# The start of the wide matmuls' operands: 96 bytes past a multiple of 128, or on one

## The chip, the cores and the metric

The kernel runs on one core of a Trainium2 chip. A core has a matrix engine (TensorE, in the profile PE, with its weight loads as PEld), VectorE (DVE), ScalarE (ACT), GpSimd (POOL) and SyncE (SP), which issues nearly all transfers. The metric is the device time of one execution in microseconds.

## What is computed

One layer of a decoder trunk over 2048 tokens of width 1024, in float32. An input projection feeds two groups of token mixers (four heads of a gated delta rule, four of HGRN2, each with 128 x 128 states); an output projection, a squared-ReLU MLP of width 4096 and a gated per-layer embedding follow, with RMS norms between:

```python
hn = rms_norm(h, pre_mix_norm[i])
proj = jnp.einsum('btd,dc->btc', hn, w_in[i])
...
o_a = gated_delta_rule_chunked(q_a, k_a, v_a, g_dec, beta)
o_b = hgrn2_chunked(jax.nn.silu(q_hg), k_b, i_hg, log_f)
...
h = h + rms_norm(jnp.einsum('btc,cd->btd', mix, w_out[i]), post_mix_norm[i])
u = jnp.einsum('btd,df->btf', rms_norm(h, pre_mlp_norm[i]), w_mlp_up[i])
y = jnp.einsum('btf,fd->btd', jnp.square(jax.nn.relu(u)), w_mlp_down[i])
h = h + rms_norm(y, post_mlp_norm[i])
e = rms_norm(jnp.einsum('bte,ed->btd', p[i], w_ple_proj[i]), ple_norm[i])
gate = jax.nn.sigmoid(jnp.einsum('btd,de->bte', h, w_ple_gate[i]))
h = h + e * gate
```

## The kernel before

Everything is held transposed, with features in the 128 partitions and tokens along a partition, 512 tokens at a time. Each large product is made from matmuls of a 128 x 128 stationary operand with a moving operand of 128 partitions by 512 columns. Both are float32r tiles that hold a number in two parts, the rounded value and the rest; three matmuls (high by high, high by low, low by high) stand for one float32 product:

```python
terms += [(w[:, 0, k, :], xk[:, 0, :]), (w[:, 0, k, :], xk[:, 1, :]), (w[:, 1, k, :], xk[:, 0, :])]
```

There are 10,344 such wide matmuls in the program, and 48 more with 256 columns in the last output tile. The rest are narrow ones in plain float32, most of them with 128 columns or fewer, in the mixers.

The stages follow one another in time. First come the embedding projection (tiles `mme`) and the norms of the first tokens. Then, up to about 1012 us, the input projection (`mm`, line 1176) runs with the mixers' narrow matmuls put in between: each of 132 projections has 24 wide matmuls in three steps of eight, and after each step a table of offsets says which part of which mixer is issued. Then the output projection (`mmo`), the MLP's up product (`u`) and down product (`d`), both in seven products instead of eight with sums on VectorE, and the gate (`mmg`), all through line 1210. TensorE's order is the order of the code; in the MLP SyncE's is too. VectorE and ScalarE prepare the split operands and take the results out of the accumulators.

Where an operand starts is decided by the pools. A pool is a stretch of each partition; pools are laid one behind another from the left, or, with `side="right"`, from the other end. Tiles are rounded up to 32 bytes, so an address is the sum of what was allocated ahead. Four pools hold the operands of wide matmuls. `ra` is a ring of ten moving tiles of 4096 bytes, behind the small constants of `cp`. `wp` holds stationary tiles at the right end while the mixers run, and `bp` takes its place in the MLP. `rb` is a second ring of 18 moving tiles, opened after the mixers where their tiles were, and the tiles of the pool `b2` (the same use as `bp`) lie behind it. A pool `pad` with one tile that nothing uses stands ahead of `rb`:

```python
cp = ctx.enter_context(tc.tile_pool(name="cp", bufs=1))                                    # 102
ra = ctx.enter_context(tc.tile_pool(name="ra", bufs=10))                                   # 103
wp = wctx.enter_context(tc.tile_pool(name="wp", bufs=3, side="right"))                     # 105
...
ctx.enter_context(tc.tile_pool(name="pad", bufs=1)).tile([P, 48], F32, name="pad")         # 1194
second.append(ctx.enter_context(tc.tile_pool(name="rb", bufs=18, reuse_waits="tile")))     # 1195
```

In the built program the first tile of `ra` starts at byte 18144 of its partition, the first of `rb` at 81888, and the stationary tiles at 204768 and the like: each is 96 bytes past a multiple of 128. The parts inside a tile start a multiple of 512 bytes further on, so all operands of the wide matmuls, stationary and moving, have that remainder.

Of the kernel before, what the change touches and what calls it, by code (L numbers as in the profile page):

```python
# [10 lines left out]
F32 = mybir.dt.float32  # L11
# [9 lines left out]
P = 128  # L21
# [75 lines left out]
def trunk(ctx, tc, x, xT, pT, vecs, w_in, w_ab, gdn_a_log, gdn_dt_bias, w_out, w_up, w_down,  # L97
# [2 lines left out]
    V, S, G, PE = nc.vector, nc.scalar, nc.gpsimd, nc.tensor  # L100

    cp = ctx.enter_context(tc.tile_pool(name="cp", bufs=1))
    ra = ctx.enter_context(tc.tile_pool(name="ra", bufs=10))
    wctx = ctx.enter_context(ExitStack())
    wp = wctx.enter_context(tc.tile_pool(name="wp", bufs=3, side="right"))
    st = ctx.enter_context(tc.tile_pool(name="st", bufs=2))
# [1084 lines left out]

    pp = ctx.enter_context(tc.tile_pool(name="pq", bufs=4, space=PSUM))
    po = ctx.enter_context(tc.tile_pool(name="pr", bufs=2, space=PSUM))
    ctx.enter_context(tc.tile_pool(name="pad", bufs=1)).tile([P, 48], F32, name="pad")
    second.append(ctx.enter_context(tc.tile_pool(name="rb", bufs=18, reuse_waits="tile")))
    f2 = ctx.enter_context(tc.tile_pool(name="f2", bufs=1, reuse_waits="tile"))
    octx = ctx.enter_context(ExitStack())
# [791 lines left out]
```

## Time and profile before

| | |
|---|---|
| median of 3 runs | 2643.54 us (2637.11 to 2644.09) |
| span of the profiled execution | 2639.5 us, 4.0 us under that median |
| TensorE busy | 2602.8 us, 15593 matmul records |
| VectorE, ScalarE, GpSimd busy | 1965.0, 1463.3, 137.0 us |
| moved by DMA | 573.87 MB, 217 GB/s on the mean |

The span goes from the first to the last instruction of the profiled execution. The profile gives no time of that execution beside it; the timed runs stand in the first row. Busy time of TensorE counts from each matmul's start to a modelled end, and neighbouring matmuls overlap, so the time that one costs is read from the distance between starts. A plain float32 matmul appears as two records, a float32r one as one.

### The profile page before, as it was taken

What the parts mean: (1) busy time and instruction counts of PE and PEld (TensorE: products, weight loads), DVE (VectorE), ACT (ScalarE), POOL (GpSimd) and SP (SyncE); (2) the same over time, 40 slices, a digit from 0 to 9 for tenths busy, and PEclk for the clock granted to TensorE, in tenths of its full rate; (3) what the DMA queues carried; (4) which work ended last, traced back from release to release, by engine and by line L of the source; (5) the groups of instructions that cost most, each with busy time, mean ns of one, the idle gap of its engine ahead of it and who ended that gap; (6) DMA issues with size and microseconds to landing.
All of it is one profiled execution on the core that took longest, in us unless ns stands there. A gap on an engine that the chain in (4) does not pass through costs nothing.

```text
span 2639.5 us, 43913 instructions
## 1 busy us (share of the span) xinstructions
PE 2602.8 (99%) x15593; PEld 2146.0 (81%) x15593; DVE 1965.0 (74%) x4032; ACT 1463.3 (55%) x2991; POOL 137.0 (5%) x147
## 2 busy tenths in 40 slices
PE   8999999999999999999999999999999999999999
PEld 6778788878878888787888888888888888888887
DVE  7778777776777777579988768767877765477775
ACT  7766655465555555566666465555454465565431
POOL 0000000000000000110000000001000001101000
PEclk9999999999999999999999999999999999999999
DMA  8877777767767675764675576665644375677663
GB/s 277 282 258 265 263 256 245 238 222 251 241 213 240 222 237 162 232 203 141 214 236 182 179 233 223 214 211 186 220 150 168 140 245 187 202 252 251 207 223 126
DMA packets 267788, 573.87 MB, mean 217 GB/s; under 512 B 55578, under 2 KB 60152, under 8 KB 250416
## 3 DMA queue, kind: packets, MB, share of 16 engines
q1 hardware_dynamic: 265264, 566.86, 64.5%
q0 software_dynamic: 2304, 4.20, 0.9%
q8 instruction: 123, 2.02, 0.3%
q14 instruction: 97, 0.79, 0.1%
HBM read 410.57 MB, written 160.37 MB: 216 GB/s over the span
## 4 chain that ended last, share of the span: by engine, by line
PE 61%; DMA 2%; issue 2%; DVE 2%; ACT 0%; POOL 0%; SPq 0%; DVEq 0%; POOLq 0%; ACTq 0%
PE d L1210 23%; PE u L1210 23%; PE mmg L1210 7%; PE mm L1176 4%; PE mmo L1059 1%; PE mme L203 1%; DMA yod<-yo 1%; DMA mixT<-mixd 0%; DMA rsb_g<-rd_g 0%; DMA yo<-in_xT_dram 0%; DVE t L177 0%; DMA rd_g<-m_g 0%; DVE acc_o L246 0%; POOL yo L1296 0%; DMA raw_out<-in_w_out_dram 0%
## 5 line engine op out<-in xcount | busy, mean ns | idle before, releaser
L1176 PE MATMUL mm<-xt,w 128*128 128x512 f32 x3072 | 785.5, 401 | 1.6 <-DVE acc_vg L571 0.7
L1176 PEld LDWEIGHTS mm<-xt,w 128*128 128x128 f32 x3072 | 552.8, 188 | 108.3 <-issue 2.1
L1210 PE MATMUL d<-db,da 128*128 128x512 f32 x2688 | 612.8, 389 | 0.0
L1210 PE MATMUL u<-t,wu 128*128 128x512 f32 x2604 | 591.2, 389 | 0.0
L1210 PEld LDWEIGHTS d<-db,da 128*128 128x128 f32 x2688 | 504.5, 188 | 104.8
L1210 PEld LDWEIGHTS u<-t,wu 128*128 128x128 f32 x2604 | 488.7, 188 | 101.5
L230 DVE TENSOR_TENSOR db<-db 128x512 fp32r<-128x512 f32 x224 | 159.5, 712 | 60.0 <-ACT db L229 59.0
L1612 DVE TENSOR_TENSOR u<-u,u 128x512 f32<-128x512 f32 x224 | 150.2, 681 | 52.0 <-PE u L1210 50.4
L229 ACT ACTIVATE db<-db 128x512 fp32r<-128x512 f32 x224 | 140.9, 629 | 67.4 <-DMA db<-hid 63.6
L1210 PE MATMUL mmg<-h2T,wg 128*128 128x512 f32 (+1 forms) x792 | 174.7, 383 | 0.0
L1210 PEld LDWEIGHTS mmg<-h2T,wg 128*128 128x128 f32 x792 | 145.5, 188 | 29.1
L1655 ACT ACTIVATE u<-u 128x512 f32<-128x512 f32 x128 | 80.7, 631 | 152.8 <-DVE u L1612 152.1
L177 DVE TENSOR_TENSOR da<-da 128x512 fp32r<-128x512 f32 x128 | 95.2, 743 | 91.3 <-ACT da L176 89.5
L176 ACT ACTIVATE da<-da 128x512 fp32r<-128x512 f32 x128 | 80.6, 630 | 127.8 <-DMA da<-sumd 100.9
L1210 PE MATMUL mmo<-mixT,w_out 128*128 128x512 f32 x600 | 140.0, 393 | 3.3 <-ACT w_out L176 2.0
L1210 PEld LDWEIGHTS mmo<-mixT,w_out 128*128 128x128 f32 x600 | 113.4, 190 | 28.8 <-DVE w_out L177 2.6
L176 ACT ACTIVATE wu<-a 128x512 fp32r<-128x512 f32 x124 | 75.0, 623 | 55.8 <-DMA a<-in_w_up_dram 52.9
L177 DVE TENSOR_TENSOR wu<-a,wu 128x512 fp32r<-128x512 f32 x124 | 85.9, 694 | 8.3 <-ACT wu L176 8.2
L177 DVE TENSOR_TENSOR da<-dr,da 128x512 fp32r<-128x512 f32 x96 | 68.2, 711 | 23.7 <-ACT da L176 22.2
L1656 ACT ACTIVATE u<-u 128x512 f32<-128x512 f32 x128 | 80.4, 628 | 3.0
L176 ACT ACTIVATE da<-dr 128x512 fp32r<-128x512 f32 x96 | 60.5, 630 | 31.9 <-DMA dr<-in_w_down_dram 21.7
L246 POOL TENSOR_TENSOR acc_y<-acc_y,sq_y 128x512 f32<-128x512 f32 x28 | 37.8, 1351 | 759.5 <-ACT sq_y L245 759.5
(401 smaller groups left out, 3675.4 us busy)
## 6 DMA issues: line engine op xcount, KB each, us to landing
w<-cache_in SPq DMA_DIRECT2D x96, 1024.0 KB
db<-hid SPq DMA_DIRECT2D x224, 256.0 KB
cache_in<-w SPq DMA_DIRECT2D x32, 1024.0 KB
hid<-u SPq DMA_DIRECT2D x128, 256.0 KB
da<-sumd SPq DMA_DIRECT2D x128, 256.0 KB
a<-in_w_up_dram SPq DMA_DIRECT2D x124, 256.0 KB
hid<-ht SPq DMA_DIRECT2D x96, 256.0 KB
dr<-in_w_down_dram SPq DMA_DIRECT2D x96, 256.0 KB
```

The lines of the kernel that those rows point to most:

```text
L176: S.activation(t[:, 0], raw, AF.Copy)
L177: eng.tensor_tensor(t[:, 1], raw, t[:, 0], ALU.subtract)
L203: PE.matmul(ps, a, b, start=i == 0, stop=i == n - 1)
L229: S.activation(t[:, 0], plain(t), AF.Copy)
L230: V.tensor_tensor(t[:, 1], plain(t), t[:, 0], ALU.subtract)
L246: eng.tensor_tensor(acc, acc, sq, ALU.add)
L1059: PE.matmul(ps, w[:, term // 2, k, :], xin[q][k][:, term % 2, :], start=i == 0, stop=i == 3 * KD - 1)
L1176: PE.matmul(ps, *terms[i], start=i == 0, stop=i == nt - 1)
L1210: PE.matmul(ps, a, b, start=start, stop=stop)
L1612: V.tensor_tensor(c[new], c[old], ps, ALU.add)
L1655: S.activation(c[k], c[k], AF.Relu)
L1656: S.activation(c[k], c[k], AF.Square)
```

## The change

A tile of 32 bytes is added to `cp`, ahead of `ra`; a tile of 96 bytes is put at the right end, ahead of `wp`; and the tile of `pad` shrinks from 192 to 64 bytes. Nothing reads or writes these tiles. Every other allocation keeps its size and order.

```diff
     cp = ctx.enter_context(tc.tile_pool(name="cp", bufs=1))
+    cp.tile([P, 8], F32, name="even")
     ra = ctx.enter_context(tc.tile_pool(name="ra", bufs=10))
+    ctx.enter_context(tc.tile_pool(name="edge", bufs=1, side="right")).tile([P, 24], F32, name="edge")
     wctx = ctx.enter_context(ExitStack())
...
-    ctx.enter_context(tc.tile_pool(name="pad", bufs=1)).tile([P, 48], F32, name="pad")
+    ctx.enter_context(tc.tile_pool(name="pad", bufs=1)).tile([P, 16], F32, name="pad")
```

In the built program `ra` now starts at byte 18176, `rb` at 81792, and the stationary tiles named above at 204672, all multiples of 128. What lies between `ra` and `rb` (the tiles of the mixers, the norms and the staging) moves up by 32 bytes with `ra`. The instructions, their order on each engine and the semaphores that they wait for are the same.

## The prediction

> **What bounds the kernel now.** I read the page's head and busy shares first, then the list of what TensorE waits for, then the groups of its instructions, and then its instructions in order of time, to get the distance from one matmul to the next. The page says that TensorE is the bound nearly everywhere, at a granted clock of nine tenths or more in every slice:
>
> ```profile
> span 2639.5 us, 43913 instructions
> PE 2602.8 (99%) x15593; PEld 2146.0 (81%) x15593; DVE 1965.0 (74%) x4032; ACT 1463.3 (55%) x2991; POOL 137.0 (5%) x147
> PEclk9999999999999999999999999999999999999999
> ```
>
> The span leaves 36.7 us in which TensorE ran nothing. The list of its waits opens with one at the very start (pT), and falls to a few microseconds at once; the last column is the longest single wait:
>
> ```profile
> PE mme L203 <- ACT pT L176: 9.4, 2, 7.1
> PE of_g L633 <- ACT y_qg L580: 2.5, 3, 1.0
> PE mmo L1210 <- ACT w_out L176: 2.0, 1, 2.0
> PE psa_g L820 <- DVE S_g L832: 1.9, 4, 0.6
> ```
>
> So a change in the time per matmul reaches the end of the kernel, and a change elsewhere doesn't. Nearly all of that work is one shape, 128 rows by 512 columns. The groups by shape (count, busy us, mean ns, idle before):
>
> ```profile
> L1176 PE MATMUL mm<-xt,w 128*128 128x512 f32 x3072 | 785.5, 401 | 1.6 <-DVE acc_vg L571 0.7 <-DVE w L177 0.5 <-DVE acc_kg L571 0.4
> L1210 PE MATMUL d<-db,da 128*128 128x512 f32 x2688 | 612.8, 389 | 0.0
> L1210 PE MATMUL u<-t,wu 128*128 128x512 f32 x2604 | 591.2, 389 | 0.0
> L1210 PE MATMUL mmg<-h2T,wg 128*128 128x512 f32 x744 | 169.0, 389 | 0.0
> L1210 PE MATMUL mmo<-mixT,w_out 128*128 128x512 f32 x600 | 140.0, 393 | 3.3 <-ACT w_out L176 2.0 <-DVE w_out L177 1.3
> L633 PE MATMUL of_g<-y_kg 128*32 128x96 f32 x64 | 7.3, 248 | 0.0
> L952 PE MATMUL pss_h<-v_h,hk_h 128*128 128x128 f32 x128 | 16.9, 275 | 0.0
> L1210 PE MATMUL mmg<-h2T,wg 128*128 128x256 f32 x48 | 5.9, 283 | 0.0
> ```
>
> The mean of 389 ns is the time from a matmul's start to its modelled end; neighbours overlap, so it isn't the price. The price is the distance between starts. Three merged rows of the instructions in order of time give it (start us, us from first start to last end, count at the end):
>
> ```profile
> 1661.80 38.47 PE L1210 MATMUL d<-db,da 128*128 128x512 f32 x169
> 2629.21 5.91 PE L1210 MATMUL mmg<-h2T,wg 128*128 128x256 f32 x48
> 140.19 1.06 PE L952 MATMUL pss_h<-v_h,hk_h 128*128 128x128 f32 x8
> ```
>
> Take off the last one's own duration and divide by the number of steps: 512 columns (38.47 - 0.389) / 168 = 226.7 ns; 256 columns (5.91 - 0.283) / 47 = 119.7 ns; 128 columns of plain float32 (1.06 - 0.275) / 7 = 112.1 ns.
>
> **The change, part by part.** It adds or removes no instruction and no wait; it moves tiles by 32 bytes up (everything allocated from the left before the second ring), by 96 bytes down (the second ring and what follows it, and everything allocated from the right). In the built programs all 10,344 matmuls of 512 columns (9,708 in the five groups above, 636 in smaller ones), and the 48 of 256, start at 96 past a multiple of 128 bytes before and at a multiple after, with both of their operands. The two new tiles are never written or read, and cost nothing: no engine and no DMA touches them.
>
> *The wide matmul.* From 256 to 512 columns the distance grows by 107.0 ns, so a column costs 0.418 ns. 512 columns would then take 214.0 ns and 256 columns 107.0 ns: both widths show the same 12.7 ns on top. What could those be? A run of 2048 bytes that starts 96 bytes past a multiple of 128 touches 17 pieces of 128 bytes, a run of 1024 bytes touches 9; from a multiple of 128 they touch 16 and 8. One piece is 32 columns, 32 x 0.418 = 13.4 ns. If a matmul that takes one column per step can't hide the piece that it reads too much, both widths pay about 13 ns, which is what they show; pieces of 64 bytes would make 33 instead of 32, or 6.7 ns, and that isn't what stands there. The third row agrees: plain float32 takes 275 - 248 = 27 ns for 32 columns, 0.84 ns each, half the pace; at that pace five pieces for four (67 ns) hide under 107 ns of columns, and only 112.1 - 107.0 = 5.1 ns remain, less than half of the 12.7. So I take the extra piece for real. What the trace can't show is what is left when it is gone. Bounds: nothing left (saving 12.7 ns, the whole remainder), or the 5.1 ns of the narrow matmul, the nearest row of a matmul that isn't held by its reads (saving 7.6 ns). Neither row is nearer; I take the middle, some 2.5 ns left, a saving of 10.2 ns.
>
> [...]
>
> Sum: 10,344 x 10.2 ns = 105.5 us, and 48 x 10.2 ns = 0.5 us, together 106 us; at the ends 10,392 x 12.7 = 132 us and 10,392 x 7.6 = 79 us. The weight loads (81% busy, beside the matmuls) get the same shift; they are hidden, 188 ns inside 226.7, and stay inside 216:
>
> ```profile
> L1210 PEld LDWEIGHTS d<-db,da 128*128 128x128 f32 x2688 | 504.5, 188 | 104.8
> ```
>
> I count nothing for them, and nothing for the narrow matmuls. If that cover went, the excess of a load over a matmul would come on top, and there is none as long as the distance stays above 188 ns.
>
> *What is given back.* With TensorE faster, what was just in time is late. Two stages decide:
>
> ```profile
> 88.00:1020.00 932.00, 919.69 (x7977) 759.63 (x7975) 711.22 (x2051) 539.61 (x1422) 53.12 (x61) 1.00 0.73 243
> 1188.00:1452.00 264.00, 262.68 (x1157) 216.56 (x1156) 236.13 (x382) 161.76 (x273) 0.00 (x0) 1.00 0.58 193
> 1254.00:1320.00 66.00, 66.00 (x293) 54.63 (x292) 61.51 (x102) 40.06 (x67) 0.00 (x0) 1.00 0.65 215
> 2000.00:2270.00 270.00, 270.00 (x1193) 1.00 0.56 188
> ```
>
> (Columns: stretch, its us, then busy us and count of PE, PEld, DVE, ACT and POOL, the clock, the share of the DMA engines, GB/s; the last row is of PE alone.) The first is the mixers. There 396 steps of 8 wide matmuls stand between the narrow ones, which wait for VectorE and ScalarE in a chain. Each step gets 8 x 10.2 = 82 ns shorter. TensorE is idle 932 - 919.7 = 12.3 us there, in short waits like those listed above, so few steps wait today, but some do. If in one step of four the result comes after the shortened step, 99 x 82 ns = 8 us are given back. The bounds are 0 and the whole 32 us of these steps. The second is the start of the MLP: VectorE is busy 236.1 of 264 us there, 27.9 us over for 382 instructions, 73 ns each. In its fullest part, 1254 to 1320 us, 61.5 of 66 us are busy and 4.5 us lie between 102 instructions, 44 ns each; I take that as what it needs. TensorE would want this part in 66 - 293 x 0.0102 = 63.0 us, VectorE can't do it under 66.0, so 3 us are given back; over the whole stretch TensorE wants 252.2 us and VectorE 236.1 + 382 x 0.044 = 252.9, about even. Bounds 0 and all 12 us. After 1452 us VectorE has room (the last row's stretch: TensorE without a gap, and 10.2 ns of 226.7 is 4.5%). The transfers:
>
> ```profile
> GB/s 277 282 258 265 263 256 245 238 222 251 241 213 240 222 237 162 232 203 141 214 236 182 179 233 223 214 211 186 220 150 168 140 245 187 202 252 251 207 223 126
> DMA packets 267788, 573.87 MB, mean 217 GB/s; under 512 B 55578, under 2 KB 60152, under 8 KB 250416
> ```
>
> In a span 4% shorter 217 GB/s become 226, and the first slices already hold 277 to 282; I count nothing for them.
>
> 106 - 11 = 95 us. On the profile's span: 2639.5 - 95 = 2544.5 us; the median of the runs, 2643.54, is 4.0 us above that span, and I keep the 4.0: **2548.5 us**, 3.6% less.
>
> **The rivals.** *More is given back.* If the mixers keep their pace (32 us lost) and the stage from 1188 to 1452 too (12 us), 62 us remain: 2581.5 us; with the small end of the saving, 79 - 44 = 35 us: 2608. For it speaks that the mixers' narrow matmuls stand in a chain through three engines, one after another; against it, that VectorE is busy only 711 of 932 us there (76%), and that the waits listed come to few microseconds.
>
> *No change.* The 12.7 ns belong to every wide matmul, whatever its address: the change of the weights, say, costs a fixed time. For it: it is the same at both widths, and all wide matmuls before have one alignment, so that the trace has no other to compare. Against it: a fixed price per instruction should show on the narrow ones, which load weights for each matmul as well, and those show 5.1 ns. It gives 2643.5 us, within 0.3%. [...]
>
> *Slower.* The same shift moves the operands of VectorE and ScalarE. If an address class that is good for TensorE is bad for VectorE, its instructions get longer, and the place where that decides is the stretch from 1188 to 1452 us: it has 73 ns for each of 382 instructions there. Above that VectorE is the bound: at 100 ns more each, 382 x 0.027 = 10 us there and, with no gain on TensorE, 2654 us. Against it: it would take 15% of an instruction of 681 ns, the commonest one there, and TensorE without a gain:
>
> ```profile
> L1612 DVE TENSOR_TENSOR u<-u,u 128x512 f32<-128x512 f32 x224 | 150.2, 681 | 52.0 <-PE u L1210 50.4
> ```
>
> That the change doesn't do what it says is excluded by the addresses of the built programs, named above.
>
> **How the numbers follow.** The forecast (the piece is saved, little given back) 0.67; more given back 0.13; no change 0.14; slower 0.06. Runs of this kernel lie between 2637.1 and 2644.1 us, so 0.3% is about what can be told from no change. The first two are faster: 0.80; same 0.14; slower 0.06. The range goes from the whole 132 us with nothing given back, 2511, a little under it for the rounding of the rows, to the far end of the second case, 2608: 2508 to 2608 us. That leaves out the last two cases, 2 in 10.
>
> **What would show it.** In the profile after, the run of d-matmuls should show 214 to 219 ns from start to start instead of 226.7, the 256-column ones 107 to 112 instead of 119.7, and the plain float32 ones no change within 2 ns. The stretch from 2000 to 2270 us should hold some 1250 matmuls instead of 1193. The mean of VectorE's and ScalarE's instructions should stay, their shares rise by 3 to 4%. TensorE's idle time should grow from 36.7 us to some 48, in the mixers above all. I am wrong on the cause if the distance stays at 226.7 ns, wrong on the size if it comes out under 214 or above 219, and wrong on what is given back if the sum of TensorE's waits grows by more than 20 us or not at all.

## The result, and the profile after

The changed kernel takes 2657.26 us (median of 4 runs, 2655.01 to 2659.55), the kernel before 2643.82 (4 runs, 2637.11 to 2644.60): 1.0058 times as long, with an interval of 1.0041 to 1.0074. It is slower by about 0.6%; forecast was a gain of 3.6%. The head of the page after shows where it went, in the same lines as before:

```profile
span 2655.9 us, 43913 instructions
PE 2622.1 (99%) x15593; PEld 2145.2 (81%) x15593; DVE 1963.3 (74%) x4032; ACT 1465.0 (55%) x2991; POOL 137.4 (5%) x147
PEclk9999999999999999999999999999999999999999
```

The span grew by 16.4 us, TensorE's busy time by 19.3 us, at the same granted clock (0.999 and 1.000 on the mean) and with the same instructions; VectorE and ScalarE stayed within 2 us. So TensorE is still the bound, and its own work got longer. The groups by shape tell which part (count, busy us, mean ns, idle before; lines lie 2 further down than before):

```profile
L1178 PE MATMUL mm<-xt,w 128*128 128x512 f32 x3072 | 795.6, 404 | 1.2 <-DVE acc_vg L573 0.9 <-DVE acc_qg L573 0.2
L1212 PE MATMUL d<-db,da 128*128 128x512 f32 x2688 | 613.1, 389 | 0.0
L1212 PE MATMUL u<-t,wu 128*128 128x512 f32 x2604 | 599.3, 392 | 0.0
L1212 PE MATMUL mmg<-h2T,wg 128*128 128x512 f32 x744 | 170.6, 391 | 0.0
```

`mm` went from 785.5 to 795.6 us and `u` from 591.2 to 599.3, while `d`, with nearly as many matmuls of the same shape, stayed (612.8 to 613.1). The change put all operands on multiples of 128 bytes, so alignment alone can't divide `u` from `d`. Distances from start to start, as in the prediction (runs of `u` before, then of `d` and `u` after, in order of time):

```profile
1840.41 38.92 PE L1210 MATMUL u<-t,wu 128*128 128x512 f32 x171
```
```profile
1666.66 43.68 PE L1212 MATMUL d<-db,da 128*128 128x512 f32 x192
1850.51 38.79 PE L1212 MATMUL u<-t,wu 128*128 128x512 f32 x168
```

`u` before: (38.92 - 0.389) / 170 = 226.7 ns. After: `d` (43.68 - 0.389) / 191 = 226.7 ns, `u` (38.79 - 0.392) / 167 = 229.9 ns. No run of wide matmuls fell below 226.7 ns, and some became slower.

What divides them are the pools, seen modulo 256 instead of 128. Before, every wide operand starts 224 bytes past a multiple of 256. After, the first ring `ra` (18176) starts on a multiple of 256, and the stationary tiles (204672) and the second ring `rb` (81792) 128 past one. The moving operand lies in `ra` for all matmuls of `mm` and for a part of `mmo`, `u`, `mmg` and `mme` (960 of the 2688 of `u`); but for 48 of `mme`, whose weights lie in `ra` too, their two operands are now 128 bytes apart, modulo 256. The operands of `d`, and those of the matmuls fed from `rb`, still have equal starts. The experiments test whether this distance is the cause.

### The profile page after: what moved, and what is told of

Same layout as the page of the kernel before. It is cut to its first block, busy times and chain, and to the rows that moved or that the text cites. A ratio compares the mean times of both kernels' runs of the same rounds, so it can differ in the third digit from the quotient of the medians.

```text
span 2655.9 us, 43913 instructions
## 1 busy us (share of the span) xinstructions
PE 2622.1 (99%) x15593; PEld 2145.2 (81%) x15593; DVE 1963.3 (74%) x4032; ACT 1465.0 (55%) x2991; POOL 137.4 (5%) x147
## 4 chain that ended last, share of the span: by engine, by line
PE 68%; DVE 3%; DMA 3%; issue 2%; ACT 1%; SPq 0%; POOL 0%; DVEq 0%; ACTq 0%; POOLq 0%
PE u L1212 23%; PE d L1212 23%; PE mm L1178 9%; PE mmg L1212 7%; PE mmo L1061 1%; PE mme L205 1%; DMA yod<-yo 1%; DMA mixT<-mixd 0%; DMA sys_g<-ud_g 0%; DVE t L179 0%; DVE acc_o L248 0%; PE psb_g L827 0%; PE psa_g L822 0%; DMA yo<-in_xT_dram 0%; PE of_g L836 0%
## 5 line engine op out<-in xcount | busy, mean ns | idle before, releaser
L1178 PE MATMUL mm<-xt,w 128*128 128x512 f32 x3072 | 795.6, 404 | 1.2 <-DVE acc_vg L573 0.9
L1212 PE MATMUL d<-db,da 128*128 128x512 f32 x2688 | 613.1, 389 | 0.0
L1212 PE MATMUL u<-t,wu 128*128 128x512 f32 x2604 | 599.3, 392 | 0.0
L1614 DVE TENSOR_TENSOR u<-u,u 128x512 f32<-128x512 f32 x224 | 150.2, 681 | 60.6 <-PE u L1212 59.6
```

The costliest lines, as they stand in the source:

```text
L1178: PE.matmul(ps, *terms[i], start=i == 0, stop=i == nt - 1)
L1212: PE.matmul(ps, a, b, start=start, stop=stop)
L1614: V.tensor_tensor(c[new], c[old], ps, ALU.add)
```

## Experiments

The theories: *piece*, the prediction's (only each start's place within 128 bytes counts, and the kernel lost its gain elsewhere); *place* (a start has a good or bad place modulo 256 by itself); *pair* (the distance between the starts of the moving and the stationary operand counts, modulo 256). Below, "distance" is the start of the stationary operand minus that of the moving one, modulo 256.

**The price by start, by itself.** A kernel that only multiplies: 64 groups of 25 float32r matmuls of 512 columns, the moving operand starting at m x 32 bytes, the stationary one at s x 32 bytes, m and s from 0 to 7 (letters a to h in the names).

```diff
+    PE.matmul(ps, sta[:, 8 * s : 8 * s + P], mov[:, 8 * m : 8 * m + QT], start=i == 0, stop=i == n - 1)
```

> Leaves the whole computation out: 64 groups of 25 wide float32r matmuls, the moving operand starting 0, 32, ... 224 bytes past a multiple of 256 (letter a to h after m) and the stationary one likewise (letter after s), nothing beside them. Pair theory (the distance between the two starts modulo 256 sets the price): 226.7 ns from start to start in the 8 groups where both letters are equal, some 233 ns where they are four letters (128 bytes) apart, whatever the first letter; others unknown, between 214 and 240. Place theory (a moving operand that begins on a multiple of 256 is slow): the groups of ma are slow (233 ns) with every stationary start, those of mh at 226.7 with every one. Piece theory of the prediction (an extra 128-byte piece): ma and me at 214 to 219, all others 226.7.

Its instructions in order of time (start us, us, name with m and s, count):

```profile
21.29 5.84 PE L36 MATMUL masa<-mov,sta 128*128 128x512 f32 x25
26.96 5.99 PE L36 MATMUL masb<-mov,sta 128*128 128x512 f32 x25
...
44.47 5.97 PE L36 MATMUL mase<-mov,sta 128*128 128x512 f32 x25
50.28 6.00 PE L36 MATMUL masf<-mov,sta 128*128 128x512 f32 x25
...
206.86 6.00 PE L36 MATMUL mesa<-mov,sta 128*128 128x512 f32 x25
212.69 6.00 PE L36 MATMUL mesb<-mov,sta 128*128 128x512 f32 x25
...
230.10 5.84 PE L36 MATMUL mese<-mov,sta 128*128 128x512 f32 x25
235.78 5.99 PE L36 MATMUL mesf<-mov,sta 128*128 128x512 f32 x25
```

A group's price is the step from its start to the next one's over 25. Both at 0 (masa): (26.96 - 21.29) / 25 = 226.8 ns. Stationary 128 bytes further (mase): (50.28 - 44.47) / 25 = 232.4. With the moving one at 128, `mesa`, distance 128 again, takes 233.2, and `mese`, distance 0, 227.2. By distance, the mean of the steps within a group, over the eight groups of that distance (they differ by 1.2 ns at most):

```
distance, bytes    0     32     64     96    128    160    192    224
ns per matmul    226.7  233.1  233.4  233.9  232.3  233.4  229.2  233.3
```

All eight pairs of equal start show 226.7 ns, 96 past a multiple of 128 like 0 past one. That ends *piece* and *place*; *pair* holds.

**Shapes, and two-byte operands.** The same with fewer stationary or moving columns, at distance 0 (at) and 128 (off), and in bf16.

```diff
+    group(f"{tag}_sta_{name}", sta[:, :k], mov[:, m : m + QT])    # k = 128, 96, 64, 32
+    group(f"{tag}_mov_{name}", sta[:, :P], mov[:, m : m + k])     # k = 384, 256, 128
+    group(f"bf_{tag}_{name}", stah[:, :k], movh[:, m : m + QT])
```

> Leaves the whole computation out: groups of 32 matmuls with 128, 96, 64 and 32 stationary columns at 512 moving columns, with 384, 256 and 128 moving columns, and bf16 ones, each with both starts equal modulo 256 (at) and 128 bytes apart (off). What are the 12.7 ns above the columns' time? If the weight load takes them: 226.7 ns with 128 stationary columns, about 223 with 96, 220 with 64, 217 with 32. If it is a fixed price of a float32r matmul: 226.7 with all of them, and 173, 120 and 66 ns with 384, 256 and 128 moving columns. bf16 groups: 216 ns at 512 columns if the price belongs to four-byte operands, 227 if to every matmul. Pair theory: the off groups of float32r are 5 to 8 ns slower with 128 stationary columns, less so with fewer.

In order of time:

```profile
21.76 7.42 PE L39 MATMUL at_sta_full<-mov,sta 128*128 128x512 f32 x32
...
43.74 7.57 PE L39 MATMUL at_sta_some<-mov,sta 128*32 128x512 f32 x32
51.15 5.72 PE L39 MATMUL at_mov_c<-mov,sta 128*128 128x384 f32 x32
56.71 3.99 PE L39 MATMUL at_mov_b<-mov,sta 128*128 128x256 f32 x32
60.53 3.69 PE L39 MATMUL at_mov_a<-mov,sta 128*128 128x128 f32 x32
64.06 7.66 PE L39 MATMUL off_sta_full<-mov,sta 128*128 128x512 f32 x32
...
113.66 7.09 PE L39 MATMUL bf_at_half<-movh,stah 128*64 128x512 bf16 x32
...
127.69 7.09 PE L39 MATMUL bf_off_half<-movh,stah 128*64 128x512 bf16 x32
```

Less the last one's own duration (389, 394, 334, 282, 273, 397 and, for both bf16 rows, 380 ns), over 31 steps: 512 columns 226.8 ns, 384 columns 173.7, 256 columns 119.6, so 0.42 ns per column and some 13 ns on top at each width; 128 columns 110 ns, where the columns would make 53 and the expectation had 66. So something else holds a matmul of 128 columns with its weight load at about 110 ns; the narrow plain float32 rows of the prediction show nearly the same (112.1), though that both meet one limit is not shown. At distance 128, 512 columns take 234.3 with the first, slower ones counted; 384 take 176.0 and 256 take 118.6 (mean of the steps), so with fewer moving columns the distance costs less or nothing. bf16 takes 216.5 at either distance, the value that the expectation gave for a price that belongs to four-byte operands. What else missed: a smaller weight load should have cost less, by the expectation, but 32 stationary columns take (7.57 - 0.394) / 31 = 231.5 ns, more than 128. So the 13 ns aren't a price per stationary column. With 96, 64 or 32 of them the distance hardly counts: 230 to 232 ns at both.

**All starts equal, on multiples of 128.** The kernel with the alignment that the change was to give, and equal starts modulo 256 (128 past a multiple everywhere).

```diff
+    cp.tile([P, 40], F32, name="even")
     ra = ctx.enter_context(tc.tile_pool(name="ra", bufs=10))
+    ctx.enter_context(tc.tile_pool(name="edge", bufs=1, side="right")).tile([P, 24], F32, name="edge")
...
-    rows = cp.tile([N_ROWS, P], F32, name="rows")
...
         es = ectx.enter_context(tc.tile_pool(name="es", bufs=1))
+        rows = es.tile([N_ROWS, P], F32, name="rows")
```

(The 512 bytes of `rows` in `cp` make room for the new tiles; `pad` keeps its 192 bytes.)

> All operands of wide matmuls on multiples of 128, as in the changed kernel, but all of them at 128 modulo 256, so that moving and stationary starts agree modulo 256 everywhere (one table of 512 bytes is moved to a pool of the first stage to make room). Pair theory: 2638 to 2648 us, no different from before, 226.7 ns in all stages. Place theory with multiples of 128 being slow: 2654 to 2660 us; with multiples of 256 being slow: 2638 to 2648. Piece theory: 2540 us.

2639.69 us (12 runs, 2632.88 to 2642.97) against 2641.92 of the kernel before (17 runs): ratio 0.9990 (0.9982 to 0.9999), which is within the 0.3% counted as no change. Its groups read like those before the change:

```profile
L1178 PE MATMUL mm<-xt,w 128*128 128x512 f32 x3072 | 785.4, 401 | 1.3 <-DVE acc_vg L573 1.1
L1212 PE MATMUL d<-db,da 128*128 128x512 f32 x2688 | 612.8, 389 | 0.0
L1212 PE MATMUL u<-t,wu 128*128 128x512 f32 x2604 | 591.2, 389 | 0.0
```

A multiple of 128 neither helped nor harmed: `mm`, `d` and `u` take 785.4, 612.8 and 591.2 us, where 785.5, 612.8 and 591.2 stood.

**Only the ring moved by 128 bytes.** The kernel before, all starts left at 96 past a multiple of 128, but `ra` 128 bytes further (32 columns of 4 bytes). The program differs from the one before in addresses alone.

```diff
+    cp.tile([P, 32], F32, name="even")
     ra = ctx.enter_context(tc.tile_pool(name="ra", bufs=10))
...
-    ctx.enter_context(tc.tile_pool(name="pad", bufs=1)).tile([P, 48], F32, name="pad")
+    ctx.enter_context(tc.tile_pool(name="pad", bufs=1)).tile([P, 16], F32, name="pad")
```

> The kernel before with its first ring alone moved by 128 bytes (a tile of 128 bytes ahead of it, 128 bytes less padding behind): every operand still starts 96 bytes past a multiple of 128, but first ring and stationary tiles differ by 128 modulo 256, as in the changed kernel. Pair theory: as slow as the changed kernel, 2654 to 2660 us, with 229 to 234 ns on the mean from start to start in the up product and the mixers, 226.7 in the down product. Place theory (multiples of 128 or 256 are slow): as before, 2640 to 2646 us, 226.7 ns everywhere. Other-engine theory (VectorE and ScalarE suffer from the new places): 2640 to 2646 us too.

2658.30 us (6 runs, 2652.21 to 2662.26) against 2641.92: ratio 1.0064 (1.0049 to 1.0079). That is the whole loss of the change, with the alignment of before. The groups:

```profile
L1177 PE MATMUL mm<-xt,w 128*128 128x512 f32 x3072 | 796.4, 404 | 1.4 <-ACT w L177 0.8 <-issue 0.2
L1211 PE MATMUL d<-db,da 128*128 128x512 f32 x2688 | 613.1, 389 | 0.0
L1211 PE MATMUL u<-t,wu 128*128 128x512 f32 x2604 | 599.3, 392 | 0.0
```

`u` and `d` have the busy time of the changed kernel to 0.1 us.

**Other distances.** The same edit with `ra` 64 bytes further (`even` 16, `pad` 32 columns: distance 192) and 160 bytes further (`even` 40, `pad` 8: distance 96), the cheapest and the dearest unequal distance of the table.

```diff
+    cp.tile([P, 16], F32, name="even")      # the second kernel: 40
...
+    ctx.enter_context(tc.tile_pool(name="pad", bufs=1)).tile([P, 32], F32, name="pad")      # the second kernel: 8
```

> The kernel before with its first ring alone moved by 64 bytes, so that the stationary operand starts 192 bytes past the moving one modulo 256. The bare matmuls showed 228.9 ns at this distance, against 232.4 at 128 and 226.7 at none. Pair theory: 2.2 / 5.7 of what the move by 128 bytes cost (16 us), so 6 us slower than before, 2645 to 2651 us; place theory: no change, or the same 16 us.

> The kernel before with its first ring alone moved by 160 bytes, so that the stationary operand starts 96 bytes past the moving one modulo 256, where the bare matmuls showed their worst distance, 234.3 ns. Pair theory: 7.6 / 5.7 of 16 us, so 21 us slower than before, 2658 to 2668 us; place theory: no change, or the same 16 us.

Distance 192 gives 2655.37 us (5 runs, 2651.56 to 2656.78), ratio 1.0048 (1.0034 to 1.0062): more than expected. Distance 96 gives 2660.91 (5 runs, 2656.72 to 2665.88), ratio 1.0076 (1.0063 to 1.0088), as expected; both against 2641.40 (9 runs). The groups, first of distance 192:

```profile
L1177 PE MATMUL mm<-xt,w 128*128 128x512 f32 x3072 | 790.5, 403 | 0.9 <-DVE acc_vg L572 0.4 <-DVE w L178 0.3 <-issue 0.2
L1211 PE MATMUL u<-t,wu 128*128 128x512 f32 x2604 | 601.0, 393 | 0.0
```

then of distance 96:

```profile
L1177 PE MATMUL mm<-xt,w 128*128 128x512 f32 x3072 | 799.4, 406 | 0.9 <-DVE acc_vg L572 0.9
L1211 PE MATMUL u<-t,wu 128*128 128x512 f32 x2604 | 600.6, 393 | 0.0
```

`mm` follows the table in its order: 785.5 us at distance 0, 790.5 at 192, 795.6 at 128, 799.4 at 96. `u` doesn't: 601.0 at 192, as much as at the dear distances. There matmuls of both rings alternate, so the distance changes every few matmuls, most often after three, six or nine. After a change to `rb` the equal ones start slow too: the first five in the changed kernel (229 to 235 ns, then 226.8), nine at distance 96, ten at distance 192. So the matmuls of `u` from `ra` and from `rb` take 232.2 and 229.3 ns on the mean in the changed kernel, 231.1 and 230.7 at distance 192. A long run's price can't be used for a mixture; that is where the expectation for distance 192 failed. What makes the equal ones start slow stays open: in the bare kernel all eight equal groups have 226.7 from their first step.

**The stationary tiles moved instead.** The kernel before, with 128 bytes put in at the right end, ahead of `wp`: the starts of all stationary tiles at the right change against both rings, and a part of `d` (1080 of 2688 matmuls) gets unequal starts for the first time. Both rings move down by the 512 bytes of `rows`, which leaves their remainders as they were.

```diff
+    ctx.enter_context(tc.tile_pool(name="edge", bufs=1, side="right")).tile([P, 32], F32, name="edge")
...
-    rows = cp.tile([N_ROWS, P], F32, name="rows")
...
+        rows = es.tile([N_ROWS, P], F32, name="rows")
```

> The kernel before with the right end of the partition moved down by 128 bytes, so that both rings and the two blocks of the pool b2 stay where they were and the stationary tiles at the right end move; every start stays 96 bytes past a multiple of 128 (one table of 512 bytes is moved to a pool of the first stage to make room). Now all mm matmuls, 2160 of 2688 in the up product, and 1080 of 2688 in the down product, which was untouched so far, have their two starts 128 bytes apart. Pair theory: mm as in the changed kernel (mean 232.4, 7 us longer), up product 230 to 232 ns (8 to 14 us), down product 228 to 230 ns (4 to 7 us), gate and output projection 5 to 8 us: 24 to 36 us slower than before, 2665 to 2678 us. Place theory of the moving operand: no moving operand of the first three products has moved, so no change, 2638 to 2646 us.

2672.55 us (4 runs, 2669.24 to 2675.10) against 2640.48 (7 runs): ratio 1.0127 (1.0110 to 1.0144), as expected. The group that no other kernel had touched grows:

```profile
L1211 PE MATMUL d<-db,da 128*128 128x512 f32 x2688 | 621.1, 392 | 0.0
L1211 PE MATMUL u<-t,wu 128*128 128x512 f32 x2604 | 604.0, 394 | 0.0
```

612.8 to 621.1 us for `d`, or 229.7 ns on the mean where 226.7 stood: the 1080 unequal matmuls take 232.7, the 1608 equal ones between them 227.7. `mm` has 795.8. These two pay more than was expected (8.3 us instead of 4 to 7, and 10.3 instead of 7). So for `mm`, all of it at distance 128, it doesn't matter which of the two is moved: 796.4 us with the ring moved, 795.8 with the stationary tiles.

**Fine steps, and operands that stand still.** The multiplying kernel with the stationary operand moved in steps of 4 bytes, to look for a distance better than 0.

```diff
+    group(f"s{'abcdefgh'[e // 8]}{'abcdefgh'[e % 8]}", sta[:, e : e + P], mov[:, :QT])      # e = 0 to 63
+    group("mov_still", sta[:, :P], mov[:, 0:1].broadcast_to([P, QT]))
```

> Leaves the whole computation out: 64 groups of 26 wide float32r matmuls in which the moving operand stays on a multiple of 256 bytes and the stationary one starts 0, 4, 8, ... 252 bytes past one (two letters, the second counts 4 bytes), and four groups with half the rows, a quarter of them, a moving operand that stands still in one column, and a stationary one that does. [...] If some distance not yet tried takes the 13.3 ns away, a group comes out at 214 to 219 ns. If reads by the weight load stand in the way of the moving reads, the group whose moving operand stands still comes out under 226.7 ns; if the 13.3 ns are a fixed price of the switch, it stays at 226.7.

The 13.3 ns are what 226.7 has over 512 columns at 0.4167 ns, the price of a column that the next kernel shows. In order of time, the group at 100 bytes (sdb), and the one with a still stationary operand:

```profile
172.65 6.06 PE L37 MATMUL sdb<-mov,sta 128*128 128x512 f32 x26
178.54 6.22 PE L37 MATMUL sdc<-mov,sta 128*128 128x512 f32 x26
...
430.24 6.19 PE L37 MATMUL sta_still<-mov,sta 128*128 128x512 f32 x26
436.27 6.09 PE L37 MATMUL end<-mov,sta 128*128 128x512 f32 x26
```

No distance came under 226.6 ns. 226.6 to 226.7 also stands at some places that aren't 0: at 100 bytes ((6.06 - 0.394) / 25 = 226.6), 144, 156, 204, 244 and 252, and at 120, 132 and 240 after three to six slower steps. The rest lies between 229 and 238 on the mean of a group. So equal starts are the best, but not the only ones. 4 bytes already cost 5.7 ns (232.4). Of the last groups, the one with 64 rows lasts 6.18 us, about 231 ns per matmul on the mean, and a stationary operand that stands still takes (436.27 - 430.24) / 26 = 231.9, about as much as at unequal starts. In the group with 32 rows and in the one whose moving operand stands still the granted clock fell (0.63 and 0.78 over the groups), so the still moving operand is taken up again in the next kernel.

**What of the price is reading.** The moving operand reads 4, 16 or 128 columns again and again, or one column 512 times, at distances 0, 64, 128 and 192 (letters a, c, e, g); the granted clock is 1.00 from 30 to 140 us.

```diff
+    part = bass.AP(part.tensor, part.offset, [list(part.ap[0]), [0, QT // k], [1, k]])      # k = 4, 16, 128
+    group(f"again_col_{'abcdefgh'[s]}", sta[:, 8 * s : 8 * s + P], mov[:, 0:1].broadcast_to([P, QT]))
```

> Leaves the whole computation out: wide float32r matmuls whose moving operand reads 128, 16, 4 or 1 column again and again (512 columns in all), each at stationary starts 0, 64, 128 and 192 bytes past the moving one, then one in which both operands stand still, and still ones of 384 and 256 columns. If the 13.3 ns above the columns' time and the dependence on the distance both come from reads of the weight load that meet reads of the moving stream: with 128 columns (512 bytes, twice the period) as before, 226.7 and 229 to 234 ns; with one column 217 to 220 ns at every distance, as the one still group before showed at one distance; with 4 and 16 in between. If only the dependence comes from there, and 13.3 ns are fixed: 226.7 ns with one column at every distance.

In order of time:

```profile
21.08 6.72 PE L47 MATMUL again_four_a<-mov,sta 128*128 128x512 f32 x30
...
47.32 7.42 PE L47 MATMUL again_sixteen_a<-mov,sta 128*128 128x512 f32 x30
54.57 7.43 PE L47 MATMUL again_sixteen_c<-mov,sta 128*128 128x512 f32 x30
...
104.00 6.72 PE L37 MATMUL again_col_a<-mov,sta 128*128 128x512 f32 x30
110.56 6.72 PE L37 MATMUL again_col_c<-mov,sta 128*128 128x512 f32 x30
117.12 6.72 PE L37 MATMUL again_col_e<-mov,sta 128*128 128x512 f32 x30
...
136.80 5.12 PE L37 MATMUL still_mov_c<-mov,sta 128*128 128x384 f32 x30
141.76 3.52 PE L37 MATMUL still_mov_b<-mov,sta 128*128 128x256 f32 x30
```

Steps over 30: one column again and again (110.56 - 104.00) / 30 = 218.7 ns at every distance, and the same for four columns; sixteen columns (64 bytes) again and again (54.57 - 47.32) / 30 = 241.7, dearer than any straight read, where the expectation had both in between. One column read 384 times takes (141.76 - 136.80) / 30 = 165.3, and 256 times 112.0 (steps within the group), so a column costs (218.7 - 112.0) / 256 = 0.4167 ns. With 128 columns repeated it is about the price of the straight read, 228.0 at distance 0 and 232.3 at 128 (within a group). So the price depends on what the moving operand reads; with moving reads that stay in one place the dependence on the distance goes, and 8.0 of the 13.3 ns that 226.7 has over 512 columns at 0.4167. That reads of the weight load meet reads of the moving stream is the expectation's supposition; no run shows where the price comes from. What the runs show, in float32r, is that the same 512 columns take 226.7 or 232.3 ns by where the weights start relative to the moving operand.

## Why the prediction was wrong

**What bounds the kernel** was right. TensorE is busy 99% of both spans, and a few ns per matmul reach the end.

**The step that failed** is "So I take the extra piece for real". The 12.7 ns on top were there, at both widths, and the runs show them again at three (13 ns). They don't come from where an operand starts within 128 bytes: the eight equal pairs have 226.7 ns from every start, the kernel with all starts on multiples of 128 and equal takes 2639.69 us, and the runs of `d` after the change stayed at 226.7 ns, which the prediction itself named as the sign of a wrong cause. Two things carried the step, and both were weak. The count of pieces was arithmetic that happened to give the right number. The row that seemed to agree, 5.1 ns left on the narrow matmul, can't carry it: float32r matmuls of 128 columns take 110 ns too, with equal starts, where the pace of the wide ones would give 66, so something else holds a row of 128 columns, and it says nothing about the piece. Besides, the row counts records, and a plain float32 matmul is two of them (128 records of `pss_h` for 64 matmuls), so 112.1 ns is half a matmul. The trace of before had one alignment; as the rival "no change" said, it had no other to compare, and no row of it could price this edit.

**The weight loads** were counted at nothing because they are hidden in length (188 ns inside 226.7). Their length stayed at 188 ns after the change (and it is no bound in itself: in the narrow rows of before, loads of 192 ns start 112 ns apart); the whole effect goes with where their operand starts relative to the matmul's moving one. The text asked which remainder modulo 128 each operand has, and never for the distance of the two modulo 256, which was 0 before, and after the change 128 in all of `mm` and in a part of `mmo`, `u` and `mmg`.

**The rivals.** "No change" (2643.5 us) would have been right for equal starts. But its reason, the same price whatever the address, isn't right either: the price is the same for every equal pair, and 2 to 8 ns higher for unequal ones in steps of 32 bytes. "Slower" had the sign and, with 2654 us, came nearest, but that was luck: its mechanism is another one, VectorE's operands. They didn't move the time, as the commonest of its instructions shows, on the page after:

```profile
L1614 DVE TENSOR_TENSOR u<-u,u 128x512 f32<-128x512 f32 x224 | 150.2, 681 | 60.6 <-PE u L1212 59.6
```

681 ns before and after; it now waits longer for TensorE (60.6 us instead of 52.0).

**The sum, as it came out.** Where each stage of the profiled execution starts, before and after, in us:

```
            first mm    mmo       u        d        u        d       end
before         40.0   1011.9   1213.9   1522.2   1827.3   2132.4   2639.5
after          40.9   1019.9   1220.0   1532.0   1837.1   2146.5   2655.9
longer by       0.9      7.1     -1.9      3.7      0.0      4.3      2.3
```

(The last row, from 0.9 on: the stage that ends at that column's start; the second `d` has the gate behind it.) The stages of `u` pay 8.0 us: its 960 matmuls from `ra` take 232.2 ns instead of 226.7, which makes 5.3 us, and the 1728 from `rb` 229.3 instead of 227.7, which makes 2.7. The first stage of `d` pays nothing. The mixers pay 7.1 us. The output projection's -1.9 us is no gain of the change: in the kernel with equal starts that stage is 3 us shorter than before, with the old price of a matmul.

**What is given back** in a faster kernel was not measured, since none became faster; the slower ones show the same chain with the sign turned round. The stretch of the mixers, then the short one at the start of the MLP and the late one, after:

```profile
88.00:1020.00 932.00, 922.52 (x7907) 755.50 (x7906) 703.92 (x2036) 537.08 (x1415) 53.34 (x61) 1.00 0.73 242
1188.00:1452.00 264.00, 263.12 (x1145) 214.55 (x1144) 236.64 (x383) 158.80 (x267) 0.00 (x0) 1.00 0.59 193
2000.00:2270.00 270.00, 270.00 (x1183) 221.70 (x1182) 172.93 (x262) 142.25 (x240) 12.94 (x10) 1.00 0.54 181
```

In the first, TensorE's idle time fell from 12.3 to 9.5 us. Added up over the mixers, short distances between wide matmuls (under 300 ns) grew by 10.7 us (586.2 to 596.9), and distances over 700 ns, in which TensorE waits, fell from 17.7 to 12.7 us; with a little over 1 us on all others, 7.1 us reach the end of the stage. One profile isn't enough for that fall: the kernel with equal starts has 13.7 us of such distances, at the old price. But the others lie in line with it: 15.5 at distance 192, 10.1 and 10.0 in the two others at distance 128, 5.9 at 96. With slower steps the results come in time more often. The chain that the text feared for the faster kernel works as a cushion for the slower one. In the third stretch 1183 matmuls stand instead of the 1193 of before and the 1250 of the forecast. The second holds 1145 for 1157, with VectorE at 236.6 us where it had 236.1; it never became the bound.

## What to carry to other kernels

Compare the starts of the two operands of a matmul with each other, modulo 256 bytes, before giving either a rounder address; in float32r here equal starts were worth 0.5 to 1.3% of the whole kernel, and a padding tile that looks arbitrary can be what holds that relation. A trace in which every instruction has the same property can't price that property: the scan over 64 pairs took 418 us on the chip and would have replaced the argument. A comparison row from another shape supports a reason only if one knows what bounds that shape.

## What the runs showed of the hardware

The distance between float32r matmuls of 512 columns is 226.7 ns with equal starts modulo 256 and up to 233.9 in steps of 32 bytes (mean over eight pairs); in bf16 it is 216 at every distance tried. A stationary operand of 32 columns makes the matmul slower than one of 128 (231.5 and 226.8 ns). A moving operand that repeats 64 bytes is the dearest of all (239.7 to 243.4 by distance), one that repeats 4 columns or one the cheapest (218.7). At 128 moving columns a matmul with its weight load takes 110 ns, 57 more than its columns; at 256 columns 119.6. Why the period is 256 bytes, why some odd distances also reach 226.7, why fewer stationary columns don't cost less, and what the 5.3 ns are that remain at 218.7 stays open; no run here tells.
